# Four-megabyte tiles and one compute engine in a kernel that multiplies each token by two weights

## The chip, the core and the metric

The kernel runs on one core of one Trainium2 chip. The time of a run is the device time of that core in microseconds; the time of a kernel is the median of its runs. Inputs and outputs are in HBM; the engines work on SBUF, which has 128 partitions. Sixteen DMA engines carry bytes between the two. A DMA is issued by an engine's queue, here by ScalarE (ACT) or SyncE (SP), and tells of its landing through a semaphore.

## The reference

There are 16 x 1024 tokens of 512 float32 numbers, and two weights for each token. The output holds each token twice, once multiplied by each weight. The expert indices are an input that the computation does not use.

```python
batch, seq, hidden = x.shape           # 16, 1024, 512
k = expert_indices.shape[-1]           # 2
x_expanded = x[:, :, np.newaxis, :].repeat(k, axis=2)
weights = expert_weights[..., np.newaxis]
return (x_expanded * weights).astype(np.float32)
```

The input is 33.6 MB, the output 67.1 MB, the weights 0.13 MB.

## The kernel before, in words

Each partition owns 128 consecutive tokens, so the input of one partition is one run of 256 KB in HBM and its output one of 512 KB. The weights come first, in one DMA on SP (line 44), and stay.

The 128 tokens of a partition are taken in 16 iterations of `A = 8`. An input tile `t` holds 8 tokens (16 KB in a partition, 2 MB in all) and comes in two DMAs of 1 MB from the ACT queue (lines 53 and 54); there are three such tiles. The first two are loaded ahead of the loop and each iteration first issues the load of two iterations ahead. An output tile `o_tile` holds the 8 products of 4 tokens (16 KB in a partition, 2 MB); there are six, and each iteration fills two, one for each half of the input tile. Each goes out in one DMA from SP (line 93).

A product is one instruction over 128 partitions x 512 numbers with one weight in each partition. ACT makes all eight of the first half and six of the second (`nc.scalar.mul`, line 79); in the second half VectorE (DVE) makes product 0 and GpSimd (POOL) product 4 (line 85; the code also names a product 8, which does not occur). So of 256 products ACT has 224, DVE 16 and POOL 16.

Each engine works through its instructions in the order of the program. ACT's queue holds its products and the issues of the loads, SP's queue the issues of the stores. The tile framework puts in the waits: a product waits for its input to land and for its output tile to be free (its last store has landed); a store waits for its products; a load waits for the products that read the tile's former content.

Of the kernel before, what the change touches and what calls it, by code (L numbers as in the profile page):

```python
# [1 line left out]

# [4 lines left out]


@with_exitstack
def kernel(  # L10
    ctx: ExitStack,
    tc: tile.TileContext,
    x: bass.AP,
    expert_indices: bass.AP,
    expert_weights: bass.AP,
    out: bass.AP,
):
    nc = tc.nc

    batch, seq, hidden = x.shape  # L20
    k = expert_weights.shape[-1]
    P = nc.NUM_PARTITIONS
    ntok = batch * seq
    assert ntok % P == 0
    A_TOTAL = ntok // P

    xr = x.rearrange("b s h -> (b s) h").rearrange("(p a) h -> p a h", a=A_TOTAL)
    outr = out.rearrange("b s k h -> (b s) (k h)").rearrange(
        "(p a) n -> p a n", a=A_TOTAL
    )  # L30
    wr = expert_weights.rearrange("b s k -> (b s) k").rearrange(
        "(p a) k -> p a k", a=A_TOTAL
    )

    A = 8
    H = A // 2
    n_iters = A_TOTAL // A

    w_pool = ctx.enter_context(tc.tile_pool(name="w_pool", bufs=1))
    x_pool = ctx.enter_context(tc.tile_pool(name="x_pool", bufs=3))  # L40
    o_pool = ctx.enter_context(tc.tile_pool(name="o_pool", bufs=6))

    w_tile = w_pool.tile([P, A_TOTAL, k], mybir.dt.float32)
    nc.sync.dma_start(out=w_tile, in_=wr)

    x_tiles = {}

    def issue_load(j):
        if j >= n_iters:
            return  # L50
        t = x_pool.tile([P, A, hidden], mybir.dt.float32)
        a0 = j * A
        nc.scalar.dma_start(out=t[:, 0:H, :], in_=xr[:, a0 : a0 + H, :])
        nc.scalar.dma_start(out=t[:, H:A, :], in_=xr[:, a0 + H : a0 + A, :])
        x_tiles[j] = t

    issue_load(0)
    issue_load(1)

    for it in range(n_iters):  # L60
        a0 = it * A
        issue_load(it + 2)
        x_tile = x_tiles.pop(it)

        for half in range(2):
            o_tile = o_pool.tile([P, H, k, hidden], mybir.dt.float32)
            base = half * H
            opc = 0
            for ai in range(base, base + H):
                for kk in range(k):  # L70
                    w_ap = w_tile[:, a0 + ai, kk : kk + 1]
                    eng = nc.scalar
                    if half == 1:
                        if opc == 0 or opc == 8:
                            eng = nc.vector
                        elif opc == 4:
                            eng = nc.gpsimd
                    if eng is nc.scalar:
                        nc.scalar.mul(  # L79
                            out=o_tile[:, ai - base, kk, :],  # L80
                            in_=x_tile[:, ai, :],
                            mul=w_ap,
                        )
                    else:
                        eng.tensor_scalar(  # L85
                            out=o_tile[:, ai - base, kk, :],
                            in0=x_tile[:, ai, :],
                            scalar1=w_ap,
                            scalar2=None,
                            op0=mybir.AluOpType.mult,  # L90
                        )
                    opc += 1
            nc.sync.dma_start(
                out=outr[:, a0 + base : a0 + base + H, :], in_=o_tile
            )


# [1 line left out]
_INS = ['x', 'expert_indices', 'expert_weights']  # L99
_OUTS = [((16, 1024, 2, 512), 'float32')]  # L100


# [23 lines left out]
```

## Time and profile before

| | |
|---|---|
| median of 4 runs | 242.64 us (242.52 to 242.76) |
| the profiled execution, time | 242.8 us |
| the profiled execution, span | 240.7 us |
| ACT busy | 140.2 us (58%), 225 instructions |
| POOL busy | 29.8 us (12%) |
| DVE busy | 7.8 us (3%) |
| moved by DMA | 100.82 MB, 419 GB/s over the span |
| loads | 32 of 1 MB, median 28.0 us from issue to landing |
| stores | 32 of 2 MB, median 24.6 us from issue to landing |

The span is what the profiler sees of the program; the time of the execution holds 2.1 us more around it. On a page of the profile, the rows of digits cut the span into 40 equal slices of 6.0 us and give a busy share in tenths; the GB/s row gives what the DMA engines moved in each. A group's row names line, engine, operation, output and inputs, shape and count, then busy time and mean duration in ns, then the idle time ahead of it and what ended it. A queue's row gives packets, MB, and the time of its packets as a share of 16 engines' span.

### The profile page before, as it was taken

The numbers are of one execution on the slowest core, as the hardware profiler recorded it, in microseconds if no ns is written. First come the engines' busy times: TensorE is split into PE (matmuls) and PEld (weight loads), VectorE is DVE, ScalarE is ACT, GpSimd is POOL, SyncE is SP. The second block draws the span as 40 slices with busy tenths as digits, with TensorE's granted clock in tenths as the row PEclk, the third lists the DMA queues.
The fourth block names the chain that finished last, engine by engine and source line by source line (L and its number), as shares of the span: only waits on it lengthen the run. The fifth ranks groups of instructions, "written<-read, shape, count | busy, mean of one in ns | idle before, by whom it ended". The sixth has DMA issues, their size and how long they took to land.

```text
span 240.7 us, 500 instructions
## 1 busy us (share of the span) xinstructions
DVE 7.8 (3%) x16; ACT 140.2 (58%) x225; POOL 29.8 (12%) x20
## 2 busy tenths in 40 slices
DVE  0000000000000000000000000000000000000000
ACT  1989873909459193672918639095490997463000
POOL 0330303002020110302003030030300203020000
DMA  7999999999999999999999999999999999999995
GB/s 257 430 361 425 433 426 441 425 427 426 430 434 425 431 426 431 429 431 431 429 430 426 437 425 431 429 429 434 429 427 431 429 430 427 433 437 434 422 430 231
DMA packets 9363, 100.82 MB, mean 419 GB/s; under 512 B 1040, under 2 KB 1168, under 8 KB 1168
## 3 DMA queue, kind: packets, MB, share of 16 engines
q1 hardware_dynamic: 4752, 67.24, 65.4%
q10 hardware_dynamic: 4608, 33.56, 33.5%
q14 instruction: 3, 0.02, 0.0%
HBM read 33.69 MB, written 67.11 MB: 419 GB/s over the span
## 4 chain that ended last, share of the span: by engine, by line
DMA 83%; ACT 3%; ACTq 0%; issue 0%
DMA t<-in_x_dram 83%; ACT o_tile L79 3%; ACTq L121 0%; ACTq L79 0%
## 5 line engine op out<-in xcount | busy, mean ns | idle before, releaser
L79 ACT ACTIVATE o_tile<-t,w_tile 128x512 f32<-128x512 f32 x224 | 138.9, 706 | 73.4 <-DMA t<-in_x_dram 71.9
L85 POOL TENSOR_SCALAR o_tile<-t,w_tile 128x512 f32<-128x512 f32 x16 | 29.6, 1849 | 187.1 <-DMA t<-in_x_dram 187.1
L85 DVE TENSOR_SCALAR o_tile<-t,w_tile 128x512 f32<-128x512 f32 x16 | 7.8, 489 | 207.9 <-DMA t<-in_x_dram 207.9
L79 ACT ACT_TABLE_LOAD x1 | 1.3, 1283 | 5.3 <-DMA w_tile<-in_expert_weights_dram 5.3
L110 POOL MEMSET const-float32-0.0<- 128x1 f32 x1 | 0.1, 98 | 0.2 <-issue 0.2
L110 POOL MEMSET const-uint8-127<- 128x1 uint8 x1 | 0.1, 102 | 0.0
L110 POOL MEMSET const-bfloat16-1.0<- 128x1 bf16 x1 | 0.1, 101 | 0.0
L110 POOL MEMSET const-float32-1.0<- 128x1 f32 x1 | 0.1, 98 | 0.0
## 6 DMA issues: line engine op xcount, KB each, us to landing
out_dram<-o_tile SPq DMA_DIRECT2D x32, 2048.0 KB, 24.6
t<-in_x_dram ACTq DMA_DIRECT2D x32, 1024.0 KB, 28.0
w_tile<-in_expert_weights_dram SPq DMA_DIRECT2D x1, 128.0 KB, 4.6
```

The lines of the kernel that those rows point to most:

```text
L79: nc.scalar.mul(out=o_tile[:, ai - base, kk, :], in_=x_tile[:, ai, :], mul=w_ap,)
L85: eng.tensor_scalar(out=o_tile[:, ai - base, kk, :], in0=x_tile[:, ai, :], scalar1=w_ap, scalar2=None, op0=mybir.AluOpType.mult,)
L110: nc = _bacc.Bacc("TRN2", target_bir_lowering=False, num_devices=1)
```

## The change

The input tile `x_tile` becomes 16 tokens (`TX = 16`, 32 KB in a partition, 4 MB) with two buffers, loaded by one DMA from ACT. The output tile becomes 8 tokens with both products (`TO = 8`, 32 KB in a partition, 4 MB) with four buffers, stored by one DMA from SP. All 256 products are `tensor_scalar` on VectorE. No load is issued ahead in the code: the first two leave at once because two tiles are free, and each later one waits until DVE has read the tile it replaces. The tensors are addressed as flat rows. SBUF for the tiles goes from 144 KB to 192 KB in a partition.

In the built program ACT holds the 8 loads and nothing else, SP the load of the weights and 16 stores, DVE the 256 products in the order of the tokens; POOL has no product left. Each queue keeps the order of the loop.

```diff
-    xr = x.rearrange("b s h -> (b s) h").rearrange("(p a) h -> p a h", a=A_TOTAL)
+    xr = x.rearrange("b s h -> (b s) h").rearrange("(p a) h -> p (a h)", a=A_TOTAL)
...
-    A = 8
-    H = A // 2
-    n_iters = A_TOTAL // A
+    TX = 16
+    TO = 8
...
-    x_pool = ctx.enter_context(tc.tile_pool(name="x_pool", bufs=3))
-    o_pool = ctx.enter_context(tc.tile_pool(name="o_pool", bufs=6))
+    x_pool = ctx.enter_context(tc.tile_pool(name="x_pool", bufs=2))
+    o_pool = ctx.enter_context(tc.tile_pool(name="o_pool", bufs=4))
...
-        nc.scalar.dma_start(out=t[:, 0:H, :], in_=xr[:, a0 : a0 + H, :])
-        nc.scalar.dma_start(out=t[:, H:A, :], in_=xr[:, a0 + H : a0 + A, :])
...
-    issue_load(0)
-    issue_load(1)
-
-    for it in range(n_iters):
-        a0 = it * A
-        issue_load(it + 2)
...
-            o_tile = o_pool.tile([P, H, k, hidden], mybir.dt.float32)
...
-                    eng = nc.scalar
-                    if half == 1:
-                        if opc == 0 or opc == 8:
-                            eng = nc.vector
-                        elif opc == 4:
-                            eng = nc.gpsimd
...
-                        nc.scalar.mul(
...
+    for i in range(A_TOTAL // TX):
+        x_tile = x_pool.tile([P, TX * hidden], f32)
+        nc.scalar.dma_start(
+            out=x_tile, in_=xr[:, i * TX * hidden : (i + 1) * TX * hidden]
+        )
+        for j in range(TX // TO):
+            o_tile = o_pool.tile([P, TO * row], f32)
+            for t in range(TO):
+                at = (j * TO + t) * hidden
                 for kk in range(k):
+                    c = (i * TX + j * TO + t) * k + kk
+                    o = t * row + kk * hidden
+                    nc.vector.tensor_scalar(
+                        out=o_tile[:, o : o + hidden],
+                        in0=x_tile[:, at : at + hidden],
+                        scalar1=w_tile[:, c : c + 1],
+                        scalar2=None,
+                        op0=mybir.AluOpType.mult,
+                    )
+            first = (i * TX + j * TO) * row
+            nc.sync.dma_start(out=outr[:, first : first + TO * row], in_=o_tile)
```

More of the change, by code (lines that the diff above doesn't have):

```diff
@@ L25 @@
     A_TOTAL = ntok // P
-    xr = x.rearrange("b s h -> (b s) h").rearrange("(p a) h -> p a h", a=A_TOTAL)
+    xr = x.rearrange("b s h -> (b s) h").rearrange("(p a) h -> p (a h)", a=A_TOTAL)
     outr = out.rearrange("b s k h -> (b s) (k h)").rearrange(
-        "(p a) n -> p a n", a=A_TOTAL
+        "(p a) n -> p (a n)", a=A_TOTAL
     )
     wr = expert_weights.rearrange("b s k -> (b s) k").rearrange(
-        "(p a) k -> p a k", a=A_TOTAL
+        "(p a) k -> p (a k)", a=A_TOTAL
     )
-    A = 8
@@ L36 @@
-    H = A // 2
-    n_iters = A_TOTAL // A
+    f32 = mybir.dt.float32
+    row = k * hidden
+    TX = 16
+    TO = 8
     w_pool = ctx.enter_context(tc.tile_pool(name="w_pool", bufs=1))
-    x_pool = ctx.enter_context(tc.tile_pool(name="x_pool", bufs=3))
-    o_pool = ctx.enter_context(tc.tile_pool(name="o_pool", bufs=6))
-    w_tile = w_pool.tile([P, A_TOTAL, k], mybir.dt.float32)
+    x_pool = ctx.enter_context(tc.tile_pool(name="x_pool", bufs=2))
+    o_pool = ctx.enter_context(tc.tile_pool(name="o_pool", bufs=4))
@@ L44 @@
+    w_tile = w_pool.tile([P, A_TOTAL * k], f32)
     nc.sync.dma_start(out=w_tile, in_=wr)
[L46 to L52, printed above, removed]
-        nc.scalar.dma_start(out=t[:, 0:H, :], in_=xr[:, a0 : a0 + H, :])
-        nc.scalar.dma_start(out=t[:, H:A, :], in_=xr[:, a0 + H : a0 + A, :])
-        x_tiles[j] = t
-    issue_load(0)
-    issue_load(1)
-    for it in range(n_iters):
-        a0 = it * A
-        issue_load(it + 2)
-        x_tile = x_tiles.pop(it)
-        for half in range(2):
-            o_tile = o_pool.tile([P, H, k, hidden], mybir.dt.float32)
-            base = half * H
-            opc = 0
-            for ai in range(base, base + H):
-                for kk in range(k):
-                    w_ap = w_tile[:, a0 + ai, kk : kk + 1]
-                    eng = nc.scalar
-                    if half == 1:
-                        if opc == 0 or opc == 8:
-                            eng = nc.vector
-                        elif opc == 4:
-                            eng = nc.gpsimd
-                    if eng is nc.scalar:
-                        nc.scalar.mul(
[L80 to L95, printed above, removed]
```

## The prediction

> **What bounds the kernel now.** I read the page first, from busy times to slices, then the chain of work that ended last, then the DMA view in stretches where only one kind of transfer runs.
>
> ```profile
> DVE 7.8 (3%) x16; ACT 140.2 (58%) x225; POOL 29.8 (12%) x20
> ...
> DMA  7999999999999999999999999999999999999995
> GB/s 257 430 361 425 433 426 441 425 427 426 430 434 425 431 426 431 429 431 431 429 430 426 437 425 431 429 429 434 429 427 431 429 430 427 433 437 434 422 430 231
> ...
> q1 hardware_dynamic: 4752, 67.24, 65.4%
> q10 hardware_dynamic: 4608, 33.56, 33.5%
> ...
> L85 DVE TENSOR_SCALAR o_tile<-t,w_tile 128x512 f32<-128x512 f32 x16 | 7.8, 489 | 207.9 <-DMA t<-in_x_dram 207.9
> ```
>
> No engine is busy for more than 58%, the DMA row is full in every slice but the first and the last, and the rate stands at about 430 GB/s. The two queues add up to 98.9% of 16 engines' span. The counts tell what a packet is: 32 stores x 128 rows of 16 KB, 128 rows of the weights and 33 x 16 semaphore writes are q1's 4752; 32 loads x 128 rows of 8 KB and 32 x 16 semaphore writes are q10's 4608. One row of a tile is one packet.
>
> The chain repeats one step, here twice of six times:
>
> ```profile
> 39.34 29.24 DMA t<-in_x_dram
> ...
> 68.60 29.24 DMA t<-in_x_dram
> ```
>
> In 29.24 us two iterations pass: 4 loads and 4 stores, 12.58 MB, 430 GB/s. The kernel is bound by its DMA engines, and only three things can move its time: what a byte costs in them, how long they run empty or slowed, and the two ends.
>
> What a packet costs, from the DMA view between 5.5 and 12 us, where only loads run, and between 222 and 237 us, where only stores do:
>
> ```profile
> DMA packets 372, 2.78 MB, mean 427 GB/s; under 512 B 33, under 2 KB 33, under 8 KB 33
> ...
> q10 hardware_dynamic: 372, 2.78, 101.0%
> ```
>
> ```profile
> DMA packets 442, 6.46 MB, mean 430 GB/s; under 512 B 48, under 2 KB 48, under 8 KB 48
> ...
> q1 hardware_dynamic: 442, 6.46, 100.5%
> ```
>
> Loads: 1.010 x 6.5 us x 16 engines over 339 packets of 8 KB, 0.309 us each once the small semaphore writes are taken off. Stores: 1.005 x 15 x 16 over 394 packets of 16 KB, 0.611 us each. Twice the bytes cost 0.302 us more, so each packet carries some 7 ns that don't depend on its size.
>
> Last, the start, by the timeline and the stretches:
>
> ```profile
> 8.47 0.49 DVE L85 TENSOR_SCALAR o_tile<-t,w_tile 128x512 f32<-128x512 f32 x1 [8.47 <-DMA t<-in_x_dram]
> 8.55 1.84 POOL L85 TENSOR_SCALAR o_tile<-t,w_tile 128x512 f32<-128x512 f32 x1 [8.12 <-DMA t<-in_x_dram]
> 11.67 13.48 SPq L93 DMA_DIRECT2D out_dram<-o_tile  x4
> 13.36 0.49 DVE L85 TENSOR_SCALAR o_tile<-t,w_tile 128x512 f32<-128x512 f32 x1 [4.40 <-DMA t<-in_x_dram]
> ```
>
> ```profile
> 5.00:13.00 8.00, 0.49 (x1) 7.64 (x12) 1.84 (x1) 1.00 1.01 427
> 12.00:17.00 5.00, 0.49 (x1) 4.24 (x8) 1.85 (x1) 1.00 1.00 344
> ```
>
> The product at 13.36 waits for the fourth load: 4 MB have landed by then. The first store is issued at 11.67; from about 13.3 on, 1.6 us later, the rate falls, and between 12 and 17 us it is 344 GB/s (last column) against 427 before. The DMA share stays at 1.00: the engines are occupied, but each packet takes longer while the first stores join. That dip costs (430 - 344) / 430 x 5 = 1.0 us, once.
>
> **The change part by part.**
>
> Fewer, longer packets, on the path. Each engine's 12.58 MB share was 32 packets of 8 KB and 32 of 16 KB; it becomes 24 of 32 KB (8 of a load, 16 of two stores). On the line through the two rows a 32 KB packet takes 0.611 + 2 x 0.302 = 1.215 us; no row shows it. Before: 32 x (0.309 + 0.611) = 29.44 us, where the chain has 29.24, so records overlap by 3 ns each. After: 24 x 1.215 = 29.16, or 29.09 with that overlap. The gain is 0.28 or 0.15 us in each of 8 such steps: 2.2 or 1.2 us. I take the middle, **-1.7**. If 32 KB packets move only as fast as 16 KB ones, just the loads gain: 16 packets' 4 to 7 ns a step, 0.5 to 0.9 us.
>
> [...]
>
> The start. The same bytes in the same queue land the first 4 MB at 13.3 (row of 13.36). Before, ACT started at 6.64 on the first megabyte; now nothing starts until all four are there. Then 16 products make the first output tile. A DVE product took 489 ns in the mean, each beside a POOL product that is now gone, so 489 is the high end of the DVE rows; ACT's 706 ns is the nearest slower row. With 0.489: 13.3 + 7.8 = 21.1, and 1.6 us from issue to effect is 22.7. Load 1, issued right behind load 0, keeps the DMA engines occupied for 9.7 us more, to 23.0. So the engines do not run empty, with 0.3 us to spare. What shrinks is the cover of the dip: the fill of the first stores, from the drop at 13.3 to the end of the low stretch near 15.7, 2.4 us, cost 1.0 us because loads flowed through most of it. With loads over at 23.0 it may cost all 2.4: growth 0 (a faster product, store earlier) to 1.4 us. I take **+0.4**, nearer the low end, because the pipeline has the same bytes to fill whether loads stand beside it or not.
>
> [...]
>
> The weights' DMA, 8 small packets in each engine between the first load's packets, landed at 5.3; packet by packet beside 32 KB ones it lands about when load 0 does. It is covered by load 0, which the first product needs anyway; without that cover it would cost one 32 KB packet, 1.2 us.
>
> ACT's 138.9 us of products, its table load and POOL's 29.6 us go, and DVE's become 256 x 0.489 = 125 us. All of it lies beside DMA: cost 0. A 4 MB output tile takes DVE 7.8 us and the DMA engines 9.7, so DVE stays ahead; if it didn't, the difference would show 16 times.
>
> Added waits. (a) Load k+2 waits for the last product on tile k; behind it on ACT stand only later loads, and DVE waits for them. By then both stores of tile k are queued or under way. (b) The first product of an output tile waits for the store four tiles back; queued behind it are all later products, then SP's stores and ACT's loads. When it waits there, three stores of 9.7 us are outstanding, against 7.8 + 1.6 to make the next one. (c) SP's stores stand in line for products alone. The early course: stores leave at 21.1, 28.9, 36.7 and 44.5, load 2 at 28.9, load 3 at 44.5. From 23.0 on that is 24 MB, 58 us, of DMA work released in 21.5 us. If loads and stores take turns packet by packet, load 2 is there by about 50, with stores 2 and 3 still outstanding. From there the backlog covers all waits: cost 0.
>
> The end. The last load now has more than its share of the turns (equal packets instead of 8 against 16 KB), so it finishes earlier, and the end is stores alone as before: the rows behind 215 us show that already. Cost 0; at most one longer packet, +0.6, in the engine that ends last.
>
> Sum: -1.7 + 0.4 = -1.3 on the profiled execution's 242.8 is 241.5. That execution stands 0.2 above the median of 242.64; against the median, **241.3**.
>
> **The rivals.**
>
> R1, the longer packet buys little: -0.7 + 0.4, 242.3, and 241.9 to 243.5 with the dip's ends. For it: only 8 and 16 KB are in the trace. Against: the two lie on a line with a fixed part.
>
> R2, DVE is too slow for the start, the case on the slower side. If a product on DVE back to back takes ACT's 0.706, the first store takes effect at 13.3 + 11.3 + 1.6 = 26.2, and the DMA engines stand empty for 3.2 us from 23.0; the second store and load 2, both issued at 35.9, just as store 0 ends, leave 1.6 more. 242.6 - 1.7 + 4.8 = 245.7. It decides from an empty time of 2.2 us (1.7 to give back, 0.5 beyond): a first tile done at 23.6, 0.64 us a product. Against: the DVE rows are all at 0.49.
>
> R3, two input tiles are too few: when stores drain before a load lands, each load from the third on exposes its 1.6 us from issue to data, 6 x 1.6 = 9.6, less 1.7: 250.5. Against: the backlog above, and SP's stores that landed 24.6 us after issue before.
>
> **How the numbers follow.** This measurement can tell 0.2% (0.5 us) from no change. My forecast 0.64, by its ends (2.2 saved and no growth, 1.2 saved and 1.4 growth) 240.4 to 242.8: of it 0.55 faster, 0.08 the same, 0.01 slower. R1 0.16: 0.03, 0.10, 0.03. R2 0.15 and R3 0.05, slower. Together faster 0.58, the same 0.18, slower 0.24. The range takes the forecast and R1, 0.80: 240.4 to 243.5; the forecast's own is 240.4 to 242.8.
>
> **What the new profile would show.** Packets: q10 with 1024 + 128 = 1152, q1 with 2048 + 128 + 17 x 16 = 2448; a store-only stretch at about 433 GB/s (R1: 430). A first DVE product near 13.3, one store issue per 16 products, the first near 21 or before. The slices from 20 to 25 us decide dip against gap: DMA share below 0.9 there is R2. In the middle a DMA row of nines; zeros there are R3. I am wrong if packets of 32 KB are slower than the line, if first stores need the loads' cover more than I took, or if DVE products lengthen back to back.

## The result and the profile after

The changed kernel takes 242.92 us (median of 28 runs, 241.05 to 244.04) against 242.72 us for the kernel before (46 runs). The ratio is 1.0003, with a 95% interval from 0.9992 to 1.0014: no difference. What did change is the spread. The runs of the changed kernel lie over 3.0 us; 43 of the 46 before lie between 242.38 and 243.11. The other three took 246.9 to 248.1 us and are left out of the ratio, as are the slowest runs in the ratios further down (of 55 more runs of the kernel before, beside the experiments, eight took 244.1 to 247.5); none of them was profiled.

From the page of the changed kernel, the DMA rows, the queues and the products. The profiled execution took 242.22 us, with a span of 240.4; it is one of the quicker ones, 0.7 us below the median of 242.92, and what a median run loses beyond it no trace shows.

```profile
DMA  7999999999999999999999999999999999999993
GB/s 275 444 436 420 431 361 425 436 431 431 436 425 436 436 436 436 431 425 436 431 436 425 420 431 436 437 420 420 436 431 436 431 436 436 436 436 436 436 431 147
...
q1 hardware_dynamic: 2448, 67.24, 65.0%
q10 hardware_dynamic: 1152, 33.55, 33.0%
...
L59 DVE TENSOR_SCALAR o_tile<-x_tile,w_tile 128x512 f32<-128x512 f32 x256 | 102.4, 479 | 105.0 <-DMA out_dram<-o_tile 75.0
```

The packet counts are the ones worked out beforehand, 2448 and 1152, so one row of 32 KB is one packet. In the middle the mean rate is 432 GB/s where it was 430 before (last column; first the stretch of before, then that of the changed kernel):

```profile
30.00:220.00 190.00, 6.36 (x13) 117.05 (x189) 24.03 (x13) 1.00 1.01 430
```

```profile
60.00:120.00 60.00, 24.19 (x61) 0.00 (x0) 1.00 1.00 432
```

The DMA row is full: the engines do not run empty. And yet the span is the same within 0.3 us. The last slice tells where to look: 147 GB/s and a 3, where before it was 231 and a 5.

Span times the sum of the queues' shares is the time that the mean DMA engine spent on packets; the rest of the span is time in which it had none, mostly at the two ends. Before: 240.7 x 98.9% = 238.1 us, and 2.6 us of rest. After: 240.4 x 98.0% = 235.6, and 4.8. By this sum the mean engine saved 2.5 us, and waited that much longer at the ends. Part of it is only counting: records of neighbouring packets overlap by some 3 ns (3 or 4 in the packet records of both traces), and each engine has 360 packets less (585 before, 225 now), which is 1.1 of the 2.5 us. The times at which the engines end, below, are free of this.

The price of a packet, from the DMA view of the changed kernel between 200 and 230 us, where only stores run:

```profile
DMA packets 446, 12.94 MB, mean 431 GB/s; under 512 B 51, under 2 KB 51, under 8 KB 51
...
q1 hardware_dynamic: 446, 12.94, 99.9%
```

0.999 x 30 us x 16 engines over 395 large packets is 1.213 us each; the line through the two rows of before gave 1.215.

The end, from the stretches of the changed kernel (length, DVE and POOL busy, clock, DMA share, GB/s):

```profile
236.60:239.30 2.70, 0.00 (x0) 0.00 (x0) 1.00 0.14 61
```

The share counts the packets that begin in the stretch: 61 GB/s over 2.7 us are five packets of 32 KB, where 16 engines at work would begin some 36. A few engines still write while the others have nothing left. Each engine writes its part of a store's semaphore when it is done with it: in both traces a DMA ends with 16 packets of 4 bytes, 9 ns each, and those of the last store begin just as an engine's last data packet ends. The times of these last 16 writes, taken from the packet records of the two traces (ns from the span's start):

```
before 237619 237833 237846 237859 237959 238015 238162 238209 238220 238299 238349 238389 238404 238446 238459 239344
after  236111 236124 236139 236254 236300 236323 236325 236401 236556 237145 237503 237511 237691 238785 239065 239290
```

This pair of rows is the whole result. The middle engine (mean of the eighth and ninth) ends at 238.21 before and 236.48 after: 1.7 us earlier, as forecast. The last engine ends at 239.34 and 239.29. The kernel ends with the last. In the changed kernel seven engines are still at work at 236.6 us, and three after 237.7.

When did the late ones fall behind? The same semaphore writes of the earlier stores tell how far the last engine was behind the middle one, in us (stores of the changed kernel, counted from 0):

```
store    0     4     6     8     10    11    12    13    14    15
behind   1.87  1.98  3.29  1.96  2.81  2.81  2.81  2.81  2.81  2.81
```

Two thirds of the distance are there when the first store has landed, at 36.7 us, just after load 2 joined the stores; in the kernel before it is 0.83 us at the first store (24.3 us). It changes again while later loads run, in both directions. From store 10 on only stores are left, and it stays the same to a few ns.

The start, from the timeline of the changed kernel:

```profile
13.49 25.42 DVE L59 TENSOR_SCALAR o_tile<-x_tile,w_tile 128x512 f32<-128x512 f32 x64 [13.49 <-DMA x_tile<-in_x_dram]
19.94 39.01 SPq L67 DMA_DIRECT2D out_dram<-o_tile  x5
```

64 products took 25.42 us, 0.40 us each from start to start; a record of one says 479 ns, so records overlap. The first store left at 19.94, with 3.1 us of load 1 still to come (its last semaphore write is at 23.04), and cost little: no slice there is below 420 GB/s. The dip came with load 2 and store 1, both issued at 26.3:

```profile
26.00:38.00 12.00, 12.00 (x31) 0.00 (x0) 1.00 1.01 394
```

Against the 432 GB/s of the later stretches, 12 x (432 - 394) / 432 = 1.06 us: the price that the dip had before (1.0), at a later place.

### The profile page after: what moved, and what is told of

Its sections match the earlier page's. It is cut to its first block, busy times and chain, and to the rows that moved or that the text cites. A ratio compares the mean times of both kernels' runs of the same rounds, so it can differ in the third digit from the quotient of the medians.

```text
span 240.4 us, 358 instructions
## 1 busy us (share of the span) xinstructions
DVE 102.4 (43%) x256; POOL 0.2 (0%) x4
## 3 DMA queue, kind: packets, MB, share of 16 engines
q1 hardware_dynamic: 2448, 67.24, 65.0%
q10 hardware_dynamic: 1152, 33.55, 33.0%
## 4 chain that ended last, share of the span: by engine, by line
DMA 52%; DVE 21%; another core or an unknown queue 12%; issue 0%; DVEq 0%
DMA out_dram<-o_tile 36%; DVE o_tile L59 21%; DMA x_tile<-in_x_dram 16%; DVEq L93 0%; DVEq L59 0%
## 5 line engine op out<-in xcount | busy, mean ns | idle before, releaser
L59 DVE TENSOR_SCALAR o_tile<-x_tile,w_tile 128x512 f32<-128x512 f32 x256 | 102.4, 479 | 105.0 <-DMA out_dram<-o_tile 75.0
```

Source lines behind the costliest of these rows:

```text
L59: nc.vector.tensor_scalar(out=o_tile[:, o : o + hidden], in0=x_tile[:, at : at + hidden], scalar1=w_tile[:, c : c + 1], scalar2=None, op0= ...
```

## The experiments

After this reading the question was what makes single engines late. The table has each run's median and, from the profiled execution, its time and when the middle and the last engine wrote their last semaphore. "Packets" are the sizes of load and store packets. The experiments ran on three chips, each batch beside the kernel before, whose median was 242.74 to 242.86 in all of them.

| run | packets, KB | time, us | ratio to before (95%) | profiled, us | middle | last |
|---|---|---|---|---|---|---|
| before | 8 / 16 | 242.72 | | 242.80 | 238.2 | 239.3 |
| changed | 32 / 32 | 242.92 | 0.9992 to 1.0014 | 242.22 | 236.5 | 239.3 |
| e1 | 16 / 32 | 259.14 | 1.0588 to 1.0681 | 260.83 | 246.4 | 257.9 |
| e2 | 16 / 16 | 241.60 | 0.9939 to 0.9964 | 241.69 | 237.4 | 238.5 |
| e3 | 32 / 32 | 245.15 | 1.0080 to 1.0108 | 244.70 | 238.4 | 241.8 |
| e4 | 8 / 16 | 244.58 | 1.0050 to 1.0099 | 243.93 | 239.1 | 240.6 |
| e5 | 16 / 32 | 249.13 | 1.0212 to 1.0290 | 250.55 | 238.1 | 247.5 |
| e6 | 32 / 16 | 241.93 | 0.9959 to 0.9979 | 242.21 | 237.7 | 239.1 |
| e7 | 32 / 32 | 245.21 | 1.0080 to 1.0125 | 245.25 | 238.5 | 242.3 |
| e8 | 16 / 16 | 247.34 | 1.0178 to 1.0218 | 246.46 | 238.0 | 243.1 |
| e9 | 16 / 32 | 250.30 | 1.0175 to 1.0338 | 247.49 | 238.9 | 244.6 |
| e10 | 32 / 32 | 240.75 | 0.9908 to 0.9949 | 240.47 | 236.0 | 237.6 |
| e11 | 16 / 16 | 243.43 | 0.9951 to 1.0022 | 241.60 | 237.3 | 238.4 |
| e12 | 16 / 16 | 247.43 | 1.0175 to 1.0228 | 247.15 | 238.0 | 243.8 |
| e13 | 8 / 16 | 245.47 | 1.0070 to 1.0124 | 246.88 | 238.3 | 243.5 |
| e14 | 32 / 32 | 244.70 | 1.0049 to 1.0099 | 243.16 | 237.8 | 240.2 |
| e15 | 32 / 32 | 181.48 | (work left out) | 181.53 | 177.2 | 178.5 |
| e16 | 8 / 8 | 243.37 | 1.0012 to 1.0033 | 243.46 | 239.1 | 240.5 |

In all 18 profiled executions the time is 2.9 to 3.5 us past the last engine's last write, while it is 4.3 to 14.4 us past the middle one's: the time goes with the last engine. A profiled execution can lie away from the median: e9 and e14 are quicker by 2.8 and 1.5 us, e11 is one of its quicker group, e1 and e13 are slower by 1.7 and 1.4.

### The order of loads and stores, or the length of the packets: e1, e2, e3, e5

In the changed kernel the load queue runs empty several times (load 5 lands at 123.9, load 6 is issued at 127.9), and some late packets stand near these places. That was the first theory.

e1, on the changed kernel:

```diff
-        nc.scalar.dma_start(
-            out=x_tile, in_=xr[:, i * TX * hidden : (i + 1) * TX * hidden]
-        )
+        for h in range(2):
+            half = TX * hidden // 2
+            nc.scalar.dma_start(
+                out=x_tile[:, h * half : (h + 1) * half],
+                in_=xr[:, i * TX * hidden + h * half : i * TX * hidden + (h + 1) * half],
+            )
```

> The changed kernel with each 4 MB load split into two DMAs of 2 MB, so that a load packet is 16 KB and a store packet stays 32 KB; all else alike. Theory T1 (engines stall where the load queue runs empty and where it fills again beside the stores): when the queues take turns, loads now get half the bytes of stores, the pace at which they are needed, so the load queue hardly runs empty, single engines no longer fall behind, and they end within about 1 us of each other: 241.3 to 241.8 us. Theory T2 (a longer packet makes each hiccup of an engine longer, whatever the turns): loads half as long, stores as long, so little changes: 242.5 to 243. Theory T3 (256 products on VectorE beside the transfers slow single engines): as the changed kernel, 242.9.

e2, e1 and this:

```diff
-            nc.sync.dma_start(out=outr[:, first : first + TO * row], in_=o_tile)
+            for h in range(2):
+                half = TO * row // 2
+                nc.sync.dma_start(
+                    out=outr[:, first + h * half : first + (h + 1) * half],
+                    in_=o_tile[:, h * half : (h + 1) * half],
+                )
```

> The changed kernel with loads and stores both split, all packets 16 KB; tiles, waits and VectorE as in the changed kernel. The turns are equal again. T1: the load queue runs empty as often as in the changed kernel, the engines end 2 to 3 us apart, and the packets cost 1.2 us more: 243.5 to 244. T2: half the packet, half the spread: about 1 us less lost at the end, 1.2 us more for packets, 242.6 to 243.0, and runs closer together than those of the changed kernel. T3: 243.5 to 244, as T1.

e3:

```diff
-    x_pool = ctx.enter_context(tc.tile_pool(name="x_pool", bufs=2))
-    o_pool = ctx.enter_context(tc.tile_pool(name="o_pool", bufs=4))
+    x_pool = ctx.enter_context(tc.tile_pool(name="x_pool", bufs=3))
+    o_pool = ctx.enter_context(tc.tile_pool(name="o_pool", bufs=3))
```

> The changed kernel with three input tiles and three output tiles in place of two and four. T1: a load is always queued behind the running one, the queue does not run empty after the start: 241.3 to 242. T2 and T3: packets and engine are the same: 242.9. If three output tiles are too few, VectorE waits on stores and the DMA row shows slices below nine; then 243 or more.

e5:

```diff
-    TX = 16
+    TX = 8
...
-    x_pool = ctx.enter_context(tc.tile_pool(name="x_pool", bufs=2))
+    x_pool = ctx.enter_context(tc.tile_pool(name="x_pool", bufs=4))
```

> Input tiles of 8 tokens (16 KB a row, 2 MB, one DMA), four of them, and four output tiles of 32 KB as in the changed kernel; all products on VectorE. The turns give loads half the bytes of stores, and up to three loads can queue. The first store can leave some 5 us earlier than in the changed kernel, while loads still run. T1: 241.0 to 241.6, engines within about 1 us at the end. T2: 242.4 to 242.9, T3: 242.9.

The first theory fell at once, and so did my sense of how large the effect could be. The three kernels that were to keep the load queue filled are the slow ones: 259.1, 245.2 and 249.1 us. e2, which was to be slower, is the only one of the four that beats the kernel before. What happened in e5 is plain in its last stretches:

```profile
240.00:247.00 7.00, 0.00 (x0) 0.00 (x0) 1.00 0.14 61
```

For 7 us on end, some two engines' worth of writing (0.14 of 16) is left; the middle engine ended at 238.1. They were not late by chance once; they ran slowly for long. The DMA view of e5 between 60 and 100 us, then between 200 and 230, where nearly all is stores:

```profile
DMA packets 782, 16.86 MB, mean 421 GB/s; under 512 B 96, under 2 KB 96, under 8 KB 96
...
q1 hardware_dynamic: 391, 11.24, 67.2%
q10 hardware_dynamic: 391, 5.62, 33.2%
```

```profile
q1 hardware_dynamic: 444, 12.91, 99.7%
q10 hardware_dynamic: 14, 0.20, 1.5%
```

Beside loads, 11.24 MB of stores are 343 packets of 32 KB in 0.672 x 40 x 16 us, 1.25 us each (the 5.62 MB of loads are 343 packets of 16 KB, one for one); without loads, 394 packets in 0.997 x 30 x 16 us, 1.21. The mean hides who pays. The packet records of e5 have no engine's name, but an engine's next packet starts some 3 ns before the last one ends, so they can be strung into 16 strings. Here are all large packets that took over 1.30 us between 64 and 75.4 us (string, start, duration in ns):

```
15  64695 1552     2  64869 1545
15  66850 1535     2  67025 1447
15  68989 1407     2  69075 1375
15  71000 1461     2  71054 1467
15  73065 1366     2  73125 1355
15  75034 1445     2  75083 1452
```

Two engines, and no other, are slowed in every store packet, at the same time, and the distance between their starts shrinks from 174 to 49 ns: they come into step and stay there. Between 38 and 113 us of e5, 76 of the 79 store packets over 1.30 us have another that starts within 0.35 us. Other strings start store packets within 20 ns of each other in the same stretch and take 1213 ns. So it is not every pair that disturbs each other. In the changed kernel itself it is mostly loads that are slowed: behind the first dip, from 38 us on, 21 load packets of 711 and five store packets of 1905 took over 1.30 us, the loads mostly within a few us of a load's start or end. That store packets in step made its late engines late is therefore not shown.

### Which side, one queue, and the parts of the change alone: e6, e7, e8, e4

e6 is the changed kernel with only the store split, the second diff of e2.

> The changed kernel with each 4 MB store split into two DMAs of 2 MB: load packets 32 KB, store packets 16 KB, all else alike. After e1 (load 16 KB, store 32 KB: 259.1), e5 (the same packets, other tiles: 249.1), e2 (both 16 KB: 241.6) and e3 (both 32 KB, more loads in flight: 245.2), T1 has fallen. Theory T4: wherever loads and stores run together, a packet of 32 KB on either side makes single engines stall. It expects 243 or more here. Theory T5: only long store packets do it; it expects 241.4 to 242.0. Theory T6: packets of unequal length are what hurts most, whichever side is longer (e1, e5 against e3); it expects 248 or more.

e7, on the changed kernel, with the loads on SP:

```diff
+    tiles = []
+
+    def load():
+        n = len(tiles)
+        if n < A_TOTAL // TX:
+            x_tile = x_pool.tile([P, TX * hidden], f32)
+            nc.sync.dma_start(
+                out=x_tile, in_=xr[:, n * TX * hidden : (n + 1) * TX * hidden]
+            )
+            tiles.append(x_tile)
+
+    load()
+    load()
     for i in range(A_TOTAL // TX):
-        x_tile = x_pool.tile([P, TX * hidden], f32)
-        nc.scalar.dma_start(
...
+        x_tile = tiles[i]
...
             nc.sync.dma_start(out=outr[:, first : first + TO * row], in_=o_tile)
+        load()
```

> The changed kernel with loads issued from SP too, two ahead, so that loads and stores of 32 KB packets stand in one queue, one DMA after the other; products, tiles and buffers as in the changed kernel. Engines then do not take turns between two queues packet by packet. If T4 holds because of the turns between queues, the stalls go and the whole gain of the longer packet appears: 240.6 to 241.4, engines ending within 1.5 us of each other. If 32 KB packets stall engines by themselves, or by reads beside writes in any order: 242.5 to 244.

e8, on the kernel before:

```diff
-        nc.scalar.dma_start(out=t[:, 0:H, :], in_=xr[:, a0 : a0 + H, :])
-        nc.scalar.dma_start(out=t[:, H:A, :], in_=xr[:, a0 + H : a0 + A, :])
+        nc.scalar.dma_start(out=t, in_=xr[:, a0 : a0 + A, :])
```

> The kernel before with the two 1 MB loads of a tile made one of 2 MB (packets of 16 KB in place of 8); products stay on ScalarE, VectorE and GpSimd, tiles as before. If e2's gain comes from the packets alone (16 packets less a step, 0.5 to 0.9 us in all): 241.6 to 242.2. If e2 gained by VectorE or by the 4 MB tiles: 242.6 to 243. The first product waits 2.5 us longer, beside loads that still run: no cost expected.

e4, on the kernel before:

```diff
-                    eng = nc.scalar
-                    if half == 1:
-                        if opc == 0 or opc == 8:
-                            eng = nc.vector
-                        elif opc == 4:
-                            eng = nc.gpsimd
+                    eng = nc.vector
```

> The kernel before with all products on VectorE, transfers and tiles untouched: one part of the change alone. T3 (VectorE's products beside the transfers slow them): 243 to 244. All other theories: 242.4 to 242.9, as before; VectorE's products near 0.40 us.

Each of these missed some expectation. e6 came out at 241.9: a long load packet beside a short store does no harm, which fits T5 and goes against T4 and T6. But T5, that only long stores hurt, does not hold alone: e8 has no packet over 16 KB and is 2% slower than before. Its end, and the store packets of e8 with the same doubled duration (the same strings as above; a free packet of 16 KB takes 611 ns):

```profile
239.00:243.00 4.00, 0.00 (x0) 0.00 (x0) 0.00 (x0) 1.00 0.11 45
```

```
 6 127260 1208    12 127287 1208
 6 142716 1208     5 142757 1208
```

Two engines that start within 27 and 41 ns of each other each take about twice the time. The partners change: 6 with 12, then 6 with 5. Four more store packets of e8 took 1208 ns, and for one of them no other slowed packet starts within 400 ns, so a partner in step is not the whole of it.

e7 shows that taking turns between two queues is not needed either: with one queue the engines end 4.7 us apart. Perhaps an engine that is behind still writes a store while others have moved on to the next load, so that loads and stores meet anyway; the records do not tell loads from stores here, since both are 32 KB in one queue.

e4 is the surprise among them. Its transfers are those of the kernel before, and yet it is 0.7% slower. Products on VectorE leave ACT's queue free, so loads are issued at other moments, and the stores with them. In its stretches there is a second dip, and before has only the one at 12 to 17 us:

```profile
80.00:86.00 6.00, 3.26 (x8) 0.00 (x0) 1.00 0.99 421
86.00:92.00 6.00, 3.26 (x8) 0.00 (x0) 1.00 1.02 373
```

6 x (421 - 373) / 421 = 0.7 us in the mean of the engines (the middle one ends 0.9 us later than before). The packet records show what happens there. Between 85.2 and 90.6 us no store packet begins: the stores have run out, and loads run alone. The next store is issued at 86.6; from 87.7 on, until its packets begin, most load packets take 400 to 900 ns in place of 309. At the start of the kernel before it is the same: issue at 11.7, long load packets from 13.3, first store packet at 15.7. It is the dip of the start once more. Whether VectorE slows packets in itself was not separated here; e2 and e6 have the same products and no such loss, which speaks against it.

### Does the place of a row in HBM matter: e9 to e12

A pair that is slowed again and again made me suspect a shared place, since all rows lie 256 KB (input) or 512 KB (output) apart; no run had shown one. In these four kernels a tile is one contiguous stretch of HBM. The weights are loaded as before, so a token meets another token's weights; the transfers and products are the same in number and size. e9 (from e5; e10 from the changed kernel, e11 from e2 and e12 from e8 in the same way, with `a=16`, `16` and `8`):

```diff
-    xr = x.rearrange("b s h -> (b s) h").rearrange("(p a) h -> p (a h)", a=A_TOTAL)
+    xr = x.rearrange("b s h -> (b s) h").rearrange("(i p a) h -> p i (a h)", p=P, a=8)
...
-        "(p a) n -> p (a n)", a=A_TOTAL
+        "(i p a) n -> p i (a n)", p=P, a=8
...
-            out=x_tile, in_=xr[:, i * TX * hidden : (i + 1) * TX * hidden]
+            out=x_tile, in_=xr[:, i, :]
...
-            first = (i * TX + j * TO) * row
-            nc.sync.dma_start(out=outr[:, first : first + TO * row], in_=o_tile)
+            first = j * TO * row
+            nc.sync.dma_start(out=outr[:, i, first : first + TO * row], in_=o_tile)
```

> e5 (249.1 us: input packets 16 KB, output packets 32 KB) with the tokens dealt out anew: a tile's 128 rows are one contiguous stretch of HBM (rows 16 and 32 KB apart) where before a row lay 256 KB (input) or 512 KB (output) from its neighbour. Same tiles, packets, buffers, order. The weights are still loaded in the old order, so tokens meet the weights of other tokens. In e5 two engines ran store packets at 1.36 to 1.6 us in place of 1.21, in step with each other, while other engines did not. Theory T7 (engines in step hit the same part of HBM because rows lie a power of two apart by 256 KB or more): the slowed packets go, 240.5 to 242. Theory T8 (engines in step slow each other by something that the address of a row does not change): 247 to 251.

> The changed kernel with contiguous tiles in the same way (input rows 32 KB apart, output rows 64 KB apart), weights of other tokens as in e9. T7: engines end within 1 us, the gain of the packets appears: 240.8 to 241.4, runs close together. T8: 242.5 to 243.5, runs spread over 2 to 3 us as those of the changed kernel.

> e2 (241.6 us: all packets 16 KB) with the same new layout, weights of other tokens. e2 had few slowed packets. T7 and T8: 241.2 to 241.9.

> e8 (247.3 us: the kernel before with loads in packets of 16 KB) with contiguous tiles in the same way (input rows 16 KB apart, output rows 32 KB apart), weights of other tokens. T7: 241.2 to 242.2. T8: 246 to 248.

The theory failed where it was to show most: e9 and e12 are as slow as e5 and e8. e10 on the other hand came out where it said, at 240.75 us: the middle engine ends at 236.0, the last at 237.6 (the first at 235.8, so they end 1.8 us apart and not within 1). In its last stretch just one packet still begins:

```profile
235.50:239.00 3.50, 0.00 (x0) 0.00 (x0) 1.00 0.02 9
```

That is 2.0 us less than the kernel before, the 1.7 forecast for the packets and a little more, from the same packets, tiles, buffers and engines as the changed kernel. So the gain of the packets can show in the time when the last engine stays close. How much of it the layout brings by itself is open: the kernel before, with its own packets, was not run with contiguous tiles. e11 fell into two groups, four runs at 241.5 to 241.7 and six at 243.4 to 243.6, one program on one chip: something differs from run to run, and that it is which engines come into step is a guess. That may also be the source of the 3 us over which the runs of the changed kernel spread; I did not profile enough of them to show it. The layout does not decide alone, and the rows were still multiples of 16 KB apart, so collisions of addresses are not ruled out.

### Who sets the time, and what the slow packets need: e13 to e16

e13, on the kernel before, behind the first loads (e14 the same rows behind the changed kernel's first load), adds a load that nobody reads, 17 rows of 4 KB, 70 KB in all. At half an 8 KB packet's 0.309 us for a row, an estimate, it is 2.6 us of one engine's time if one takes all 17, as both expectations suppose (they count 2.7), and under 0.2 us if all 16 share them.

```diff
     issue_load(0)
     issue_load(1)
+    more = w_pool.tile([17, 2, hidden], mybir.dt.float32)
+    nc.scalar.dma_start(out=more, in_=xr[0:17, 0:2, :])
```

> [...] Theory S (each engine has a fixed share of the bytes, nothing evens them out, and the slowest sets the time): 1.5 to 2.7 us more than before, less what that engine had in hand, 244 to 245.5. Theory M (the mean rate of all engines sets the time): 0.2 us more, 242.7 to 243.0.

> The changed kernel with the same extra load of 17 rows of 4 KB behind its first load. Theory S: its engines already end 3 us apart, so if the burdened engine is not the last one anyway, part of the 2.7 us is hidden: 243 to 245.6. Theory M: 243.1. If an engine that is behind is slowed further because it is behind: more than 246.

e15, on the changed kernel:

```diff
+    tiles = []
+    for i in range(2):
+        x_tile = x_pool.tile([P, TX * hidden], f32)
+        nc.scalar.dma_start(
+            out=x_tile, in_=xr[:, i * TX * hidden : (i + 1) * TX * hidden]
+        )
+        tiles.append(x_tile)
     for i in range(A_TOTAL // TX):
...
+        x_tile = tiles[i % 2]
```

> The changed kernel without its last six loads: the products of later tiles read the first two input tiles again, so their outputs are wrong; stores, products and buffers as in the changed kernel. After 23 us only stores of 32 KB packets run. If slowed packets need loads beside stores: packets all at 1.21 us, engines within 1.5 us of each other at the end, 18 transfers of 4 MB at 9.68 us and 5 to 6 us around them: 179.5 to 181.5. If packets of 32 KB stall by themselves: engines 2 to 3 us apart, 182 or more.

e16 is e2 with four parts in place of two.

> The changed kernel with loads and stores each split in four, all packets 8 KB. By the packets' price a step of 12.58 MB takes 96 x 0.306 = 29.4 us, 0.2 us more than with 16 KB, 1.9 us over the program. If the loss at the end shrinks with the packet (16 KB against 32 KB gained 1.3 us net): engines within 1 us, 242.8 to 243.6. If packet length has no part in the loss: 243.5 to 246.

e13 is the cleanest of all. 70 KB more on 100.8 MB, 0.07%, cost 2.7 us, 1.1%, by the medians. The 17 packets ran one after another, from 12.2 to 16.2 us, which is one engine: 4.0 us. Before the first stores join, at 13.2, they start every 155 ns, 2.6 us for 17, as estimated; the other 1.4 us are the dip, in which seven of them took longer. In the profiled execution, the longest of its four, the last engine ended 4.2 us later than before. The stretch from 239.5 to 243.5 of e13 has about one engine writing:

```profile
239.50:243.50 4.00, 0.00 (x0) 0.00 (x0) 0.00 (x0) 1.00 0.07 29
```

An engine that lost time early in the program did not get it back here. The records show it: from 53 us to the end of the loads, the engine that ends last writes its part of each load's semaphore 8.1 to 8.3 us after the first engine does, once every 7.315 us, the same step as the others'. Nothing evened the loss out here, as if each engine had a fixed part of every transfer. e14 lost 1.8 us against the changed kernel, within its bounds, perhaps since other engines were late already; nothing shows that a late engine is slowed further for being late.

e15: after the first loads only stores of 32 KB run, and the slow packets are gone, but for two of 1.60 and 1.57 us, each of which begins just as a packet of the instruction queue ends. Its DMA view between 60 and 160 us:

```profile
DMA packets 1494, 43.16 MB, mean 432 GB/s; under 512 B 176, under 2 KB 176, under 8 KB 176
...
q1 hardware_dynamic: 1493, 43.16, 100.0%
```

1317 large packets in 1600 engine microseconds, 1.215 each, and the engines end 1.45 us apart (177.04 to 178.49). By themselves long store packets did not stall here. The other runs agree, as far as the records tell loads from stores (e7's do not): each ends with 205 to 2940 store packets behind its last load, and at most two of these are over 1.1 times their normal length. So in these runs the slowing appears where loads and stores run side by side. e16 came in at 243.37, within what the price of 96 packets of 8 KB leaves: 2.7 us later in the middle engine than the changed kernel, but only 1.4 us between the middle and the last.

## Why the prediction was wrong, point by point

"Fewer, longer packets, on the path", -1.7: the price was right. A 32 KB packet takes 1.213 us (1.215 forecast) and the middle engine ends 1.7 us earlier. (By start-to-start times the 8 steps save 1.6 us. My -1.7 was the middle between 2.2, which counts the overlap of records as time, and 1.2, so that it came this close is partly luck.) The price held for the others too: by 306, 607 and 1209 ns from packet start to packet start, e2, before and e16 should have their engines 1.0, 1.6 and 2.9 us behind the changed kernel; the middle engine has 0.9, 1.7 and 2.7.

"The start", +0.4: too much in the mean, and in the wrong place. The products take 0.40 us from start to start, not the 0.49 of the sum (the record of one is 479 ns, where it was 489 beside POOL's); that they would be faster, the low end of this term, no run had shown. The store left 1.2 us earlier than worked out; and the dip, 1.06 us against 1.0 before, came when load 2 joined the stores: +0.1. Load 0 landed at 13.46, 13.3 forecast. What the term did not hold is that the engines came out of the dip unequally: behind it the last engine was 1.87 us behind the middle one, against 0.83 before.

Added waits, cost 0, and R3: right. The DMA row has no gap; load 2 landed at 52.0 ("by about 50"). The queues did take turns packet by packet: in the packet records of the kernel before, strung into 16 strings, 4857 of 5244 neighbouring large packets between 30 and 180 us are one of a store and one of a load. R2 is out: 0.40 us a product. R1 is out for the price, though its time, 242.3, is nearer to what came.

"The end. [...] Cost 0; at most one longer packet, +0.6, in the engine that ends last": this is the step that failed. I treated sixteen engines as one with sixteen times the rate, and looked at their ends only as a rounding of one packet. The last engine ended 2.8 us after the middle one, against 1.1 before, and those 1.7 us are the whole gain. The term I put at 0 was worth +1.7, and it did not arise at the end: the distance grew while loads and stores ran together, and the stores behind 187 us only kept it. e13 shows that one late engine sets the time. The profile before could have warned me: its own last engine ended 0.9 us after the second last. That a profile of sums (GB/s, share, mean packet) can improve while the time stands still was in none of my rivals.

What is shown: the saving is in the middle engine and not in the last (the two rows of ends); the last sets the time (e13, and all 18 profiled executions); long store packets were harmless where no loads ran (e15, 1.215 us each); store packets on two engines are slowed at the same time, to double the time of a packet in the clearest cases (1208 ns against 611 in e8; 1.37 to 1.55 us against 1.21 in e5). What stays open: why the engines of the changed kernel came apart as they did, and what two slowed engines share. A store packet beside another engine's, started within some 50 ns, is sometimes slowed and mostly not (9 of 3051 such packets of the kernel before and 2 of 1376 of the changed one took over 1.1 times the normal length); 32 KB stores beside 16 KB loads are the worst of what was run (e1, e5, e9), yet 16 KB beside 16 KB is the best in one arrangement (e2) and 2% slow in another (e8). Rows in HBM that are not multiples of 16 KB apart were not tried, nor other places of the tiles in SBUF by themselves.

The loads and stores of tiles are 1 to 4 MB per DMA in all these kernels, and the times (without e15) range from 240.8 to 259.1 us: within these sizes, the size of a DMA does not order them.

## What to carry to other kernels

This DMA-bound kernel ended with its slowest DMA engine, not with its mean rate: before pricing a change of packets, look at when the middle and the last engine end, because the distance can eat any gain of a per cent. Where loads and stores run together, small changes of tiles, buffers, layout or issue order moved this kernel between 0.7% faster (e10) and 6% slower (e1), in the slowest ones through single engines that fell behind, so such variants are to be measured in many runs, not derived. Of the kernels with the right output, the changed one with 16 KB rows per DMA (e2, 241.6 us, 0.5% faster than before in six runs on one chip) is the one to keep.

## What the runs showed that I had not expected

- Store packets on two DMA engines in step can both run at about half speed (1208 ns against 611, e8) while others run free, and a pair can stay slowed for 11 us on end and more (e5).
- Moving products from ScalarE, VectorE and GpSimd to VectorE alone, with every transfer untouched, made the kernel 0.7% slower (e4): the stores ran out once, at 85 us, and the dip of the start came a second time.
- Where loads and stores first met, the engines lost about 1 us in the mean: 1.0 before (stores join loads), 1.06 after (a load joins stores), and 0.7 when it came a second time (e4). It did not happen at every meeting: loads 5, 6 and 7 of the changed kernel each joined stores that ran alone, and no slice of 6 us there is below 420 GB/s.
- 70 KB on one DMA engine cost as much time as 1.2 MB on all (2.7 us at 430 GB/s, e13).
- VectorE's 128x512 products start every 0.40 us though each is recorded as 0.48.
